# Matmuls on different parts of TensorE's array issued as neighbours in the mixers of a hybrid layer

## Chip, cores and metric

One core of one Trainium2 chip runs the whole layer in one launch. The metric is device time in microseconds (us), the median of the runs; smaller is better.

## What is computed

One layer over 512 latent tokens and 256 context tokens of 1024 channels, batch 1, in float32: a modulated RMSNorm, one input projection of width 4480, two groups of mixers, an output projection with a gated residual, a second norm, a router over 64 experts with 8 per token, a shared expert, and a final norm. The mixers are what matters here:

```python
# RWKV-7, 8 heads of 64, both directions, per token:
sa = einsum('bhvk,bhk->bhv', s, a_t)
s = s * w_t + sa[..., None] * b_t + v_t[..., None] * k_t      # state 64 x 64 per head
y = einsum('bhvk,bhk->bhv', s, r_t)
# HGRN2, 8 heads of 64, both directions, in chunks of 32 tokens:
scores = where(causal, einsum('ik,jk->ij', q * exp(cum - ref), k * exp(ref - cum)), 0)
o = scores @ v + (q * exp(cum)) @ s_prev
# modulation of both norms and of the residual gates:
mod = silu(c) @ w_mod + b_mod                                  # 1024 x 6144
```

## The kernel before

Two heads of 64 channels make a pair of 128 partitions, and there are four pairs for each kind of mixer. RWKV-7 runs in chunks of 64 tokens: 12 chunks, of which the first 4 are context and the other 8 latent, in both directions at once.

The mixers are written as Python generators, the streams. P is the projection, S the scores of RWKV-7, I the inverses of its triangular systems, A, B and C the scans over the chunks (A takes pairs 0 and 2, B pair 1, C pair 3), H and K HGRN2 (pairs 0, 1 and pairs 2, 3), M the rest of the modulation rows, U the output projection. Each stream runs from one `yield` to the next as a step, and all streams take turns. A table, PLAN, holds for each stream priorities along its steps and the number of its steps; the framework orders the instructions of each engine by these priorities and their dependences. An engine then executes its instructions in that fixed order. A wait in TensorE's queue thus holds up whatever stands behind it, of every stream.

The places that the change touches:

- `rw_scores` (stream S, matmul on line 687). For every two chunks and each head h, a matmul pair with 64 rows (the head's partitions) and 128 columns goes to one PSUM bank; DVE masks it on line 689 into the tile SC. The two heads are two steps, and they use banks 4 and 5 in turns. There are 4 pairs x 2 directions x 6 double chunks = 48 rounds of two heads.
- `rw_chain` (A, B, C). A chunk's step has four groups: the right-hand side (line 888, 64 x 64 of the array, and line 891, 128 x 64), the solve (line 902, 64 x 64), the state (line 910), and for latent chunks the output (line 926, 128 x 128, and line 928, 128 x 64). Lines 888 and 891 run over d 0 entirely and then over d 1; line 902 likewise; lines 926 and 928 alternate.
- `hgrn_pair` (H, K). For each direction, for g in (0, 2) and each head, two groups of 128 tokens make three kinds of score matmuls in one PSUM bank: lines 1115 and 1116 use 64 rows x 128 columns, line 1118 64 x 64. DVE (line 1122) and ACT (lines 1127 and 1129) bring them to SBUF. There are 4 pairs x 2 directions x 2 values of g = 16 rounds of two heads.
- `s_mod` (M). 32 loads of 512 KB of w_mod, each 256 rows x 512 columns. Each gives two matmuls with 32 array columns (line 1203) that fill one strip of 32 partitions; the four strips of a row block follow each other over four loads.

A float32 matmul shows as two records in the trace. After the mixers come norm, router and the experts, which the change does not touch.

Of the kernel before, what the change touches and what calls it, by code (L numbers as in the profile page):

```python
# [11 lines left out]
I32 = mybir.dt.int32  # L12
# [11 lines left out]
NWL, NWR = 4, 1               # buffers for the weights of experts  # L24
LAG = 2                      # loads in flight
ONPE = range(12, 44, 2)      # blocks whose rows TensorE picks, from rows on chip; the others' come by DMA
HB = 4                       # block from which on these rows are loaded
NP = 4                       # experts whose weights come before the routing is known: they rank last
# experts by size: NONE have a block of 128 slots each, NMIX 96 slots of a block, NTWO are two to a block, and the
# smallest NMIX have the other 32 slots of the former  # L30
NONE, NMIX = 18, 10
NTWO = 64 - NP - NONE - 2 * NMIX
# pairs in the output projection, in the order in which they are ready
OUT = [[('rw', 0), ('hg', 0)], [('rw', 1), ('rw', 2)], [('hg', 1), ('hg', 2)], [('hg', 3), ('rw', 3)]]
# priorities of the streams along their steps, and the number of steps; smaller ones go first
PLAN = {'W': (5, 195, 454, 106), 'P': (76, 299, 531, 185), 'E': (31, 271, 489, 172), 'O': (31, 126, 188, 169),
# [10 lines left out]
def hybrid_layer(ctx, tc, x, c, xctx, c_ctx, w_mod, b_mod, norm1_g, norm2_g, w_in, rw_conv, rw_w0, rw_w2,  # L47
# [29 lines left out]
    # ---------------------------------------------------------------- constants  # L77
# [24 lines left out]
    # masks of the chunk scores, rows (B s | K s) for d 0 and (K s | B s) for d 1, columns (A t | R t)  # L102
# [11 lines left out]
    # scan resets  # L114
# [6 lines left out]
    # masks of the 32-token blocks of HGRN2, for two heads  # L121
# [15 lines left out]
    hTh = hp.tile([128, 8, NT], FR)             # hT = hTh + hTl, each exact in float32r  # L137
# [14 lines left out]
    # conditioning vectors, then per-channel vectors, rows of 128 turned into columns  # L152
# [13 lines left out]
    lo = const.tile([128, 2, 8], F32)          # lb, 1 - lb  # L166
# [9 lines left out]
    def vectors():  # L176
# [34 lines left out]
    # adaLN: silu of the conditioning vectors as a stationary operand  # L211
# [55 lines left out]
    def banks(names):  # L267
        """PSUM in turns"""
        names = list(names)

        def get(name):
# [1630 lines left out]
```

## Time and profile before

| | |
|---|---|
| median of 3 runs | 1969.67 us (1947.13 to 1979.79) |
| span of the profiled execution | 1964.3 us |
| TensorE (PE) busy | 1777.6 us, 90% |
| DVE, ACT, POOL busy | 753.9, 618.5, 395.2 us |
| mean granted TensorE clock | 0.904 |

The profile is one execution. A row of the timeline gives the start in us, the time from the start to the last end in us, engine, line, operation, operands, shape and count; the next row's start tells when the engine came to other work. "64*128 64x128" means that 64 rows and 128 columns of the array are used and that 128 columns stream through.

### The profile page before, as it was taken

The numbers are of one execution on the slowest core, as the hardware profiler recorded it, in microseconds if no ns is written. First come the engines' busy times: TensorE is split into PE (matmuls) and PEld (weight loads), VectorE is DVE, ScalarE is ACT, GpSimd is POOL, SyncE is SP. The second block draws the span as 40 slices with busy tenths as digits, with TensorE's granted clock in tenths as the row PEclk, the third lists the DMA queues.
The fourth block names the chain that finished last, engine by engine and source line by source line (L and its number), as shares of the span: only waits on it lengthen the run. The fifth ranks groups of instructions, "written<-read, shape, count | busy, mean of one in ns | idle before, by whom it ended". The sixth has DMA issues, their size and how long they took to land. (4 is left out here: it accounts for less than half of the span.)

```text
span 1964.3 us, 25497 instructions
## 1 busy us (share of the span) xinstructions
PE 1777.6 (90%) x9675; PEld 1004.8 (51%) x9675; DVE 753.9 (38%) x1722; ACT 618.5 (31%) x1286; POOL 395.2 (20%) x372
## 2 busy tenths in 40 slices
PE   5998989999699999898999889988899999799983
PEld 2766676675577775564455443333344443433431
DVE  4566685847563344433446332111121121111113
ACT  5463535345143353421323232111121221111121
POOL 2233223313221242231230012100111110101111
PEclk9977988998579977687999989999899999899987
DMA  7313555554565354533437877995967999758975
GB/s 257 94 50 108 148 137 147 174 137 134 129 210 144 114 185 139 169 128 124 141 124 281 296 259 245 333 348 204 318 204 249 311 324 335 247 187 296 350 238 161
DMA packets 200252, 401.65 MB, mean 204 GB/s; under 512 B 41804, under 2 KB 132009, under 8 KB 175168
## 3 DMA queue, kind: packets, MB, share of 16 engines
q1 hardware_dynamic: 188768, 360.05, 53.0%
q0 software_dynamic: 11360, 39.96, 9.1%
q8 instruction: 77, 1.26, 0.3%
q14 instruction: 47, 0.39, 0.1%
HBM read 323.66 MB, written 73.15 MB: 202 GB/s over the span
## 5 line engine op out<-in xcount | busy, mean ns | idle before, releaser
L1467 PE MATMUL p_gu<-wgu,xT 128*64 128x512 f32 (+3 forms) x1104 | 424.1, 605 | 0.4 <-ACT xT L1458 0.4
L1467 PEld LDWEIGHTS p_gu<-wgu,xT 128*64 128x64 f32 (+3 forms) x1104 | 129.1, 155 | 254.0 <-issue 240.2
L1485 PE MATMUL p_y<-wd,at 128*64 128x512 f32 (+3 forms) x584 | 240.8, 636 | 4.4 <-ACT at L1480 3.0
L369 PE MATMUL p_proj<-hTh,w_hi 128*128 128x512 f32 (+1 forms) x456 | 181.5, 398 | 6.0 <-ACT w_hi L296 3.1
L370 PE MATMUL p_proj<-hTh,w_lo 128*128 128x512 f32 (+1 forms) x456 | 176.3, 388 | 3.8 <-DVE w_lo L298 3.8
L371 PE MATMUL p_proj<-hTl,w_hi 128*128 128x512 f32 (+1 forms) x456 | 177.3, 390 | 2.3 <-POOL hTl L351 1.7
L1687 POOL DMA_INDIRECT acc<-rows,li x46 | 74.3, 1616 | 463.6 <-DVE rows L1686 443.4
L1634 DVE SCALAR_TENSOR_TENSOR li<-lv,bpr 128x2 int32<-128x2 f32 x46 | 10.1, 219 | 401.1 <-DMA acc<-rows,li 287.9
L1485 PEld LDWEIGHTS p_y<-wd,at 128*64 128x64 f32 (+3 forms) x584 | 71.2, 162 | 141.8 <-issue 124.0
L1472 ACT ACTIVATE sl<-p_gu 128x256 f32<-128x256 f32 x50 | 19.2, 384 | 384.9 <-PE p_gu L1467 383.4
L1458 ACT ACTIVATE xT<-p_xg,sh2c,s2c 128x128 f32<-128x128 f32 x240 | 90.1, 461 | 110.0 <-PE p_xg L1746 109.7
L1686 DVE SCALAR_TENSOR_TENSOR rows<-p_y,lv,g2r 128x512 f32<-128x512 f32 x92 | 68.2, 746 | 147.3 <-PE p_y L1485 147.1
L369 PEld LDWEIGHTS p_proj<-hTh,w_hi 128*128 128x128 f32 x456 | 94.7, 208 | 28.4 <-issue 6.1
L371 PEld LDWEIGHTS p_proj<-hTl,w_hi 128*128 128x128 f32 x456 | 94.4, 207 | 21.7 <-issue 5.6
L370 PEld LDWEIGHTS p_proj<-hTh,w_lo 128*128 128x128 f32 x456 | 94.6, 208 | 19.6 <-issue 4.6
L1740 POOL DMA_INDIRECT xg<-h,li x30 | 31.4, 1047 | 346.6 <-issue 158.1
L1735 PE MATMUL p_xs<-sel,h2p 128*128 128x128 bf16 x1536 | 92.9, 219 | 0.0
L1735 PEld LDWEIGHTS <-h2p 128*128 128x128 bf16 x1536 | 87.4, 98 | 9.5 <-issue 9.2
L687 PE MATMUL p_sc<-AR,BK 64*128 64x128 f32 (+1 forms) x384 | 64.9, 341 | 20.0 <-DVE SC L689 9.1
L1458 ACT ACTIVATE xT<-p_xs,sh2c,s2c 128x128 f32<-128x128 f32 x128 | 48.2, 458 | 105.5 <-PE p_xs L1735 105.5
L1474 DVE TENSOR_TENSOR av<-sl,p_gu 128x256 f32<-128x256 f32 x50 | 30.1, 602 | 115.8 <-ACT sl L1472 115.8
L687 PEld LDWEIGHTS p_sc<-AR,BK 64*128 64x128 f32 x384 | 50.5, 228 | 41.3 <-issue 12.8
(520 smaller groups left out, 2716.8 us busy)
## 6 DMA issues: line engine op xcount, KB each, us to landing
wgu<-in_exp_w_gate_dram SPq DMA_DIRECT2D x64, 1024.0 KB, 6.7
wgu<-in_exp_w_up_dram SPq DMA_DIRECT2D x64, 1024.0 KB, 8.4
wd<-in_exp_w_down_dram SPq DMA_DIRECT2D x64, 1024.0 KB, 6.3
w_raw<-in_w_in_dram SPq DMA_DIRECT2D x35, 512.0 KB, 4.1
wm<-in_w_mod_dram SPq DMA_DIRECT2D x32, 512.0 KB, 3.8
pkt<-pk SPq DMA_DIRECT2D x24, 576.0 KB, 4.7
wm<-in_w_mod_dram SPq DMA_DIRECT2D x8, 1024.0 KB, 8.3
pk<-SC SPq DMA_DIRECT2D x32, 256.0 KB, 3.5
```

The source lines that it names most:

```text
L369: pe.matmul(o[k], wh[:, kt, :], hTh[:, kt, s], start=(kt == 0), stop=False)
L370: pe.matmul(o[k], wl[:, kt, :], hTh[:, kt, s], start=False, stop=False)
L371: pe.matmul(o[k], wh[:, kt, :], hTl[:, kt, s], start=False, stop=(kt == 7))
L687: pe.matmul(p3[:, i], bk[r, n + i, :], ar[r, n + i, 0:w], start=True, stop=True)
L1458: act.activation(dst[:, kt, :], v, AF.Identity, scale=s2c[:, kt:kt + 1], bias=sh2c[:, kt:kt + 1])
L1467: pe.matmul(pg[r], lhs(kt), w[0][:, :, kt * 256:kt * 256 + 256], start=(kt == 0), stop=(kt == 7))
L1474: dve.tensor_tensor(av.rearrange("s t p -> s p t"), sl.rearrange("s (p t) -> s p t", t=2), pg[:, 256:512].rearrange("s (p t) -> s p t", t= ...
L1485: pe.matmul(py[n][r], at[:, t * 128 + r.start:t * 128 + r.stop], w[1][:, t * 1024 + n * 512:t * 1024 + n * 512 + 512], start=(t == 0), sto ...
L1686: dve.scalar_tensor_tensor(yo[:, cs_], py[n], g, g2r[:, cs_], op0=OP.mult, op1=OP.mult)
L1687: pool.indirect_dma_start(out=ACC if two else ACC[0:NACC], in_=yo, in_offset=None, compute_op=OP.add, out_offset=bass.IndirectOffsetOnAxis ...
L1735: pe.matmul(pt[:, q * 128:q * 128 + 128], h2p[:, i, t, kt * 128:kt * 128 + 128], sel[:, t], start=(i == 0 and t == 0), stop=(i == 2 and t ...
L1740: pool.indirect_dma_start(out=xg.bitcast(F32), out_offset=None, in_=H2_d, in_offset=bass.IndirectOffsetOnAxis(ap=tok, axis=0))
```

## The change

In `rw_scores` both heads are issued in one step, alternating between the upper and the lower half of the array's rows, and then both are masked; both banks are taken in one step. In `rw_chain` the loops over head and direction are swapped on lines 888 and 902, so that neighbours use different halves; the matmuls with all 128 rows follow together. In `hgrn_pair` both heads are issued in one step, alternating by head, those of 64 x 64 last; then both are copied. In `s_mod` a load covers 512 rows x 256 columns, and each load feeds all four strips, with 256 columns streamed instead of 512, so that there are 8 records to a load instead of 4. The step counts in PLAN follow (S 345 to 249, H and K 153 to 129).

```diff
-        'S': (136, 309, 469, 345),
+        'S': (136, 309, 469, 249),     (H and K: 153 to 129)
 rw_scores:
-            for h in range(2):
-                r = slice(64 * h, 64 * h + 64)
-                p3 = pss("p_sc")[:, 0:2 * w].rearrange("p (i t) -> p i t", i=2)
-                for i in range(2):
+            p3s = [pss("p_sc")[:, 0:2 * w].rearrange("p (i t) -> p i t", i=2) for _ in range(2)]
+            for i in range(2):
+                for h, p3 in enumerate(p3s):
+                    r = slice(64 * h, 64 * h + 64)
                     pe.matmul(p3[:, i], bk[r, n + i, :], ar[r, n + i, 0:w], start=True, stop=True)
-                yield
+            yield
+            for h, p3 in enumerate(p3s):
                 dve.tensor_tensor(st[:, :, 0:na, h], ...)
-                yield
+            yield
 rw_chain:
-            for d in range(2):
-                for h in range(2):
+            for h in range(2):
+                for d in range(2):
                     pe.matmul(pR[r, o:o + 64], SC[rv, d, 0, h, :], W[rv, d, o:o + 64], ...)
-                if n:
-                    pe.matmul(pR[r, 0:128], AR[d][:, 0:64], S[:, d, :], start=False, stop=True)
+            if n:
+                for d in range(2):
+                    pe.matmul(pR[64 * d:64 * d + 64, 0:128], AR[d][:, 0:64], S[:, d, :], start=False, stop=True)
...
-            for d in range(2):
-                for h in range(2):
+            for h in range(2):
+                for d in range(2):
                     pe.matmul(pU[r, h * 64:h * 64 + 64], TT[r, h, :], Rs[r, h * 64:h * 64 + 64], ...)
...
                 for d in range(2):
-                    pe.matmul(pY[:, o:o + 64], S[:, d, :], AR[d][:, 64:128], start=True, stop=False)
+                    pe.matmul(pY[:, d * 64:d * 64 + 64], S[:, d, :], AR[d][:, 64:128], start=(d == 0), stop=False)
+                for d in range(2):
                     for h in range(2):
                         pe.matmul(pY[64 * h:64 * h + 64, ...], W[:, d, ...], SC[:, d, 1, h, :], ...)
 hgrn_pair:
             for g in (0, 2):
-                for h in range(2):
-                    pa = psg("p_ls")
-                    for i in range(2):
-                        pe.matmul(p0[:, i], ...)
-                        pe.matmul(p1[:, i], ...)
-                        pe.matmul(p2[kr_, i], ...)
-                    yield
-                    dve.copy_predicated(Pv, hgm[d], p0)
-                    yield
+                pas = [psg("p_ls") for _ in range(2)]
+                for i in range(2):
+                    for r, p0 in zip(hr_, p0s):
+                        pe.matmul(p0[:, i], ...)
+                    for r, p1 in zip(hr_, p1s):
+                        pe.matmul(p1[:, i], ...)
+                for i in range(2):
+                    for r, p2 in zip(hr_, p2s):
+                        pe.matmul(p2[kr_, i], ...)
+                yield
+                for h in range(2):
+                    dve.copy_predicated(Pg[:, g:g + 2, h, :], hgm[d], p0s[h])
+                yield
...
 s_mod:
-                m, g = 4 + i // 4, i % 4
-                wm = mo.tile([128, 2, 512], F32, name="wm2", bufs=3)
+                m, n, h = 4 + i // 4, i // 2 % 2, i % 2
+                wm = mo.tile([128, 4, 256], F32, name="wm2", bufs=3)
...
-                for kt in range(2):
-                    pe.matmul(pm[32 * g:32 * g + 32, :], sil[:, 2 * g + kt, :], wms[i][:, kt, :], ...)
+                for g in range(4):
+                    pe.matmul(pm[32 * g:32 * g + 32, n * 256:n * 256 + 256], sil[:, 4 * h + g, :], wms[i][:, g, :], ...)
```

## Rows read from the trace of the kernel before

**Rows 1.** The page: the span, and the granted TensorE clock in 40 slices.
```profile
span 1964.3 us, 25497 instructions
...
PEclk9977988998579977687999989999899999899987
```

**Rows 2.** Busy times by stretch: window, us, PE, PEld, DVE, ACT, POOL, clock, DMA, GB/s.
```profile
130.00:320.00 190.00, 172.45 (x949) 129.42 (x949) 124.43 (x201) 82.27 (x121) 51.76 (x34) 0.84 0.43 120
320.00:600.00 280.00, 252.32 (x1766) 188.57 (x1764) 180.99 (x394) 108.84 (x190) 82.60 (x71) 0.85 0.55 157
600.00:800.00 200.00, 196.80 (x1416) 139.76 (x1416) 78.89 (x183) 82.61 (x189) 49.11 (x80) 0.87 0.47 152
800.00:1000.00 200.00, 184.61 (x928) 104.55 (x929) 75.91 (x164) 61.67 (x138) 55.70 (x59) 0.83 0.39 131
```

**Rows 3.** Groups of PE by form: busy us, mean ns, idle before and what ended it.
```profile
L687 PE MATMUL p_sc<-AR,BK 64*128 64x128 f32 x256 | 41.6, 334 | 8.1 <-DVE SC L689 8.1
L687 PE MATMUL p_sc<-AR,BK 64*128 64x64 f32 x128 | 24.5, 353 | 11.9 <-POOL BK L637 4.3 <-DVE BK L638 3.5 <-ACT cv_b L447 3.1
L1203 PE MATMUL p_mod<-wm,sil 128*32 128x512 f32 x128 | 50.8, 789 | 2.6 <-DMA wm<-in_w_mod_dram 1.7 <-ACT mrow L1215 0.7 <-DVE y_rw L962 0.2
```

**Rows 4.** Timeline of PE: scores of one head alone, and of two heads together.
```profile
476.48 0.66 PE L687 MATMUL p_sc<-AR,BK 64*128 64x64 f32 x4
477.06 0.50 PE L370 MATMUL p_proj<-hTh,w_lo 128*128 128x512 f32 x1
...
404.11 0.72 PE L687 MATMUL p_sc<-AR,BK 64*128 64x128 f32 x8
404.76 0.50 PE L369 MATMUL p_proj<-hTh,w_hi 128*128 128x512 f32 x1
```

**Rows 5.** Timeline of PE: a right-hand side of the scan, then HGRN2's scores.
```profile
811.76 0.47 PE L888 MATMUL p_chain<-WvR,pktS 64*64 64x64 f32 x4
...
812.52 0.44 PE L888 MATMUL p_chain<-WvR,pktS 64*64 64x64 f32 x4
...
813.25 0.48 PE L1115 MATMUL p_ls<-e,k 64*128 64x128 f32 x2
...
814.10 0.48 PE L1115 MATMUL p_ls<-e,k 64*128 64x128 f32 x2
```

**Rows 6.** Timeline of PE: modulation rows of three loads, then a scan's output.
```profile
972.56 1.93 PE L1203 MATMUL p_mod<-wm,sil 128*32 128x512 f32 x12
974.54 0.43 PE L926 MATMUL p_chain<-pktS 128*128 128x64 f32 x2
974.91 0.34 PE L928 MATMUL p_chain<-pktS,WvR 128*64 128x64 f32 x4
975.17 0.43 PE L926 MATMUL p_chain<-pktS 128*128 128x64 f32 x2
...
975.80 1.12 PE L1269 MATMUL p_out<-wo,y_rw 128*128 128x512 f32 x2
```

**Rows 7.** Timeline of PE: four records of line 888 at the lower clock.
```profile
741.01 0.69 PE L888 MATMUL p_chain<-Wv,pkt 64*64 64x64 f32 x4
```

**Rows 8.** Timeline of PE: the first modulation rows, whose order alternates strips.
```profile
36.09 1.94 PE L332 MATMUL p_mod<-wm,sil 128*32 128x512 f32 x16
```

**Rows 9.** What empties the score banks: engine, count, ns min/median/max, first and last.
```profile
L689 DVE TENSOR_TENSOR SC<-p_sc,mks x96: 271/412/426, 128.1 to 525.4; 128x256 f32<-128x256 f32 x64, 128x128 f32<-128x128 f32 x32
...
L1122 DVE COPY_PREDICATED Pg<-hgm,p_ls x32: 440/444/448, 604.7 to 991.4; 128x256 f32<-128x256 uint8 x32
...
L1127 ACT ACTIVATE Pg<-p_ls x64: 197/215/218, 605.2 to 992.1; 32x64 f32<-32x64 f32 x64
...
L1129 ACT ACTIVATE Pg<-p_ls x32: 258/272/273, 605.6 to 992.3; 64x128 f32<-64x128 f32 x32
```

**Rows 10.** DMA issues: count, KB each, median us from issue to landing.
```profile
w_raw<-in_w_in_dram SPq DMA_DIRECT2D x35, 512.0 KB, 4.1
wm<-in_w_mod_dram SPq DMA_DIRECT2D x32, 512.0 KB, 3.8
```

More of the change, by code (lines that the diff above doesn't have):

```diff
@@ L882, in rw_chain @@
             W = loaded['W', n // 2][:, n % 2]
-            for d in range(2):
-                r = slice(64 * d, 64 * d + 64)
-                rv = slice(64 - 64 * d, 128 - 64 * d)
-                for h in range(2):
+            for h in range(2):
+                for d in range(2):
+                    r = slice(64 * d, 64 * d + 64)
+                    rv = slice(64 - 64 * d, 128 - 64 * d)
                     o = h * 64
@@ L898, in rw_chain @@
             yield
-            for d in range(2):
-                r = slice(64 * d, 64 * d + 64)
-                for h in range(2):
+            for h in range(2):
+                for d in range(2):
+                    r = slice(64 * d, 64 * d + 64)
                     pe.matmul(pU[r, h * 64:h * 64 + 64], TT[r, h, :], Rs[r, h * 64:h * 64 + 64],
@@ L924, in rw_chain @@
                 for d in range(2):
-                    o = d * 64
-                    pe.matmul(pY[:, o:o + 64], S[:, d, :], AR[d][:, 64:128], start=True, stop=False)
+                    pe.matmul(pY[:, d * 64:d * 64 + 64], S[:, d, :], AR[d][:, 64:128], start=(d == 0), stop=False)
+                for d in range(2):
                     for h in range(2):
-                        pe.matmul(pY[64 * h:64 * h + 64, o:o + 64], W[:, d, h * 64:h * 64 + 64],
-                                  SC[:, d, 1, h, :], start=False, stop=True)
+                        pe.matmul(pY[64 * h:64 * h + 64, d * 64:d * 64 + 64], W[:, d, h * 64:h * 64 + 64],
+                                  SC[:, d, 1, h, :], start=False, stop=(d == 1))
                 yield
@@ L1106, in hgrn_pair @@
             for g in (0, 2):
-                for h in range(2):
-                    r = slice(64 * h, 64 * h + 64)
-                    pa = psg("p_ls")
-                    p0 = pa[:, 0:256].rearrange("p (g i) -> p g i", g=2)
-                    p1 = pa[:, 256:384].rearrange("p (g n b) -> p g n b", g=2, n=2)
-                    p2 = pa[:, 384:512].rearrange("p (g i) -> p g i", g=2)
-                    for i in range(2):
-                        gs_ = slice((g + i) * 128, (g + i) * 128 + 128)
+                pas = [psg("p_ls") for _ in range(2)]
+                p0s = [pa[:, 0:256].rearrange("p (g i) -> p g i", g=2) for pa in pas]
+                p1s = [pa[:, 256:384].rearrange("p (g n b) -> p g n b", g=2, n=2) for pa in pas]
+                p2s = [pa[:, 384:512].rearrange("p (g i) -> p g i", g=2) for pa in pas]
+                hr_ = [slice(64 * h, 64 * h + 64) for h in range(2)]
+                for i in range(2):
+                    gs_ = slice((g + i) * 128, (g + i) * 128 + 128)
+                    for r, p0 in zip(hr_, p0s):
                         pe.matmul(p0[:, i], k0_[r, gs_], e1_[r, gs_], start=True, stop=True)
+                    for r, p1 in zip(hr_, p1s):
                         pe.matmul(p1[:, i], ke_[r, CTX + gs_.start:CTX + gs_.stop], qe4[r, g + i, odd::2, :],
                                   start=True, stop=True)
+                for i in range(2):
+                    for r, p2 in zip(hr_, p2s):
                         pe.matmul(p2[kr_, i], k2[r, g + i].rearrange("p n b -> p (n b)"),
                                   q2[r, g + i].rearrange("p n b -> p (n b)"), start=True, stop=True)
-                    yield
+                yield
+                for h in range(2):
+                    dve.copy_predicated(Pg[:, g:g + 2, h, :], hgm[d], p0s[h])
+                yield
+                for h in range(2):
                     Pv = Pg[:, g:g + 2, h, :]
-                    dve.copy_predicated(Pv, hgm[d], p0)
-                    yield
                     for n in range(2):
@@ L1126, in hgrn_pair @@
                         c0 = 64 * n + 32 * odd
-                        act.activation(Pv[r0:r0 + 32, :, c0:c0 + 32], p1[r0:r0 + 32, :, n, :], AF.Copy)
+                        act.activation(Pv[r0:r0 + 32, :, c0:c0 + 32], p1s[h][r0:r0 + 32, :, n, :], AF.Copy)
                     c0 = 32 * qsec
-                    act.activation(Pv[kr_, :, c0:c0 + 64], p2[kr_], AF.Copy)
-                    yield
+                    act.activation(Pv[kr_, :, c0:c0 + 64], p2s[h][kr_], AF.Copy)
+                yield
             for i0, i1 in ((0, 3), (3, 5)):
@@ L1197, in s_mod @@
             pm = psm("p_mod2")
-            for g in range(4):
-                i = 4 * (m - 4) + g
+            for q in range(4):
+                i, n, h = 4 * (m - 4) + q, q // 2, q % 2
                 loads(i + 2)
                 yield
-                for kt in range(2):
-                    pe.matmul(pm[32 * g:32 * g + 32, :], sil[:, 2 * g + kt, :], wms[i][:, kt, :], start=(kt == 0),
-                              stop=(kt == 1))
-                if g == 1:
+                for g in range(4):
+                    pe.matmul(pm[32 * g:32 * g + 32, n * 256:n * 256 + 256], sil[:, 4 * h + g, :], wms[i][:, g, :],
+                              start=(h == 0), stop=(h == 1))
+                if q == 1:
                     store()
```

3 lines of the change are left out of this document (2 added, 1 removed), and 4 rows, old and new, of the table PLAN.

## Prediction

> **What bounds the kernel now.** I read the page first, then the busy times by stretch, the groups of PE by form, and the timeline of PE where the touched lines run. The span is 1964.3 us [rows 1]. The touched matmuls lie between 130 and 1000 us, and there PE is the busiest engine in every stretch: 172.5 of 190, 252.3 of 280, 196.8 of 200 and 184.6 of 200 us, 806.2 of 870 [rows 2]. DVE comes next with 124.4 and 181.0 us up to 600 us (65%) and 39% after; ACT stays at 41% or less before 600 us and 36% after [rows 2]. So PE idles 64 us in all, and the reader should see that work taken from PE's queue has few other owners of the time. Two things are not in the busy share. Ends of matmuls are modelled, so a lone block is "busy" while its results drain. And the granted clock is 0.84, 0.85, 0.87 and 0.83 there: with only the levels 1.2 and 2.4 GHz, (1 - clock) x 2 of each stretch is at the lower one, 61 + 84 + 52 + 68 = 265 us of 870 [rows 2]. Four records of line 888 take 0.69 us at the lower level against 0.44 at the higher [rows 5, 7], 1.6 times as long. With 30% of the time at the lower level, a price taken at the full clock counts 1 / (0.7 + 0.3 / 1.6) = 1.13 times on average.
>
> **The change part by part.** PE's arithmetic stays; what changes is what runs side by side.
>
> *Scores of RWKV-7.* One head's four records keep PE 0.58 us until other work starts; eight records, two heads on the two row halves, keep it 0.65 us [rows 4]. Two heads thus cost what one costs. The 384 records hold PE 41.6 + 24.5 = 66.1 us [rows 3]. Afterwards, 48 rounds x 0.72 us (the eight's own time) x 1.13 = 39. Gain 27 us; some heads already run side by side, as the row with eight records shows, which is why it isn't half.
>
> *Right-hand side of the scan.* A chunk takes 813.25 - 811.76 = 1.49 us, one direction after the other; the second direction alone takes 813.25 - 812.52 = 0.73 [rows 5]. The two directions use different rows and columns on line 888 and different columns on line 891, so I let both run in 0.74. That is 0.75 x 44 chunks with a state x 1.13 = 37 us. From below it is nothing, if the two do not run together.
>
> *Solve.* Line 902 has the same small tiles, only reordered. I cost it at nothing, and the other two groups of a step cover any shift.
>
> *Output of the scan.* 975.80 - 974.54 = 1.26 us now, with four changes of shape [rows 6]: 0.37 for a record pair of line 926, 0.26 for four of line 928. Two changes fall away. Between 0 and 0.5 us I take 0.25: x 32 x 1.13 = 9 us.
>
> *HGRN2's scores.* One group of one head takes 814.10 - 813.25 = 0.85 us [rows 5], so a round of two heads and two groups takes 3.4. With the heads side by side, as the RWKV-7 scores of the same shape run now [rows 4], it is 1.7; the 64 x 64 ones go last, which saves a change of shape, so 1.5. That is 1.9 x 16 x 1.13 = 34 us. From below it is nothing.
>
> *Modulation.* 128 records hold PE 50.8 us [rows 3]. Sixteen records of 512 columns on alternating strips take 1.94 us [rows 8], 0.12 each, entry included; half the columns should take 0.06, so eight records take 0.49. From above stand the 0.72 us of eight records of line 687 [rows 4], as eight short records carry more of the entry each. I take 0.69, near that end. 32 x 0.69 x 1.13 = 25 us, a gain of 26. The gain is less where loads already joined, twelve records in 1.98 us [rows 6]; that is in the 50.8. Pieces of 1 KB instead of 2 KB change the loads little: those of w_raw, of the same 512 KB in pieces of 512 bytes, land in 4.1 us against 3.8 [rows 10]. DMA is at 0.39 to 0.47 there [rows 2], and the number of buffers, the 32 loads in SP's queue and the place of the stores among them stay.
>
> Sum: 27 + 37 + 9 + 34 + 26 = 133 us of PE's queue. How much of it reaches the end? At most all: PE waits only 64 of 870 us. At least nothing, if the scans' and HGRN2's dependences fill the room. Up to 600 us DVE would rise from 65% to about 72% (305 of 470 - 45 us), and it works in chains behind PE, so half should pass there; after 600 us nobody but PE is above 40%, and two thirds should pass. A good third of the sum lies in the first part (the scores and the first chunks of the scans), so I take 0.6 of the whole: 80 us. From the profiled 1964.3 that leaves 1884; the median of the runs is 5.4 above the profiled span, so 1890. The experts after the mixers keep their time and start earlier.
>
> **Rivals.**
>
> *Both banks at once (little change).* Until now one head's bank is emptied while the other is filled. Now a round takes both, and the next round waits for both: two masks of 0.41 us [rows 9], 48 x 0.82 = 39 us, and for HGRN2 two copies of 0.44, four of 0.215 and two of 0.272 us, 2.3 x 16 = 37 us. Everything behind the waiting matmul in PE's queue, of every stream, waits too. For it: the two masked tiles are the same two banks, and PE already waits 8.1 us for SC [rows 3]. Against it: other streams' matmuls stand between two rounds. If it holds in full, (133 - 76) x 0.6 = 34 us remain: 1935. The Trainium skill, "TensorEngine Tiling (Array Packing)", section Performance Considerations (PSUM Bottleneck), says that tiling speeds up TensorE but not the emptying of PSUM, and that the copy may become the limit. By that rule, this is the case to expect; the emptying engines at 65% and 41% do not show it yet.
>
> *The neighbours don't meet (little change).* The order comes from priorities, and other streams' matmuls may still be put between those of one step. With half of the gain gone, 133 / 2 x 0.6 = 40 us: 1930. For it: the lone head in [rows 4] shows how a block is set between others; against it, that one was a step of its own.
>
> *The clock (slower).* Falls to the lower level come in stretches of small matmuls, such as that of [rows 7], where PE changes among scan and scores without a wait. Shorter bursts with the same waits between them could leave PE less active and lengthen the 265 us. Each us more at the lower level loses 1 - 1 / 1.6 = 0.375 us. The gain of 80 is used up at 213 us more; slower by 2% (39 us) needs 317 us more, 582 of the 870, and gives 2009. Against it: the same columns in less time are more activity, not less, and the stretch with four strips at once [rows 8] lies in a slice with 0.9 of the clock [rows 1]. The Trainium skill, "TensorE: Matmul & The Clock Gate", the section on the oscillation in real kernels, tells of gaps that bring the lower clock again and again; the trace agrees that the clock falls often in the mixers, clock 0.83 to 0.87, and doesn't show which way this change moves it.
>
> **How the numbers follow.** Forecast, 1890: 0.66. Both banks, 1935: 0.14. Neighbours that don't meet, 1930: 0.09. Clock, 2009 at its deciding point: 0.11. A measurement of this kernel tells about 2% (39 us) from no change. Faster by more: the 0.66 and 0.02 of the banks' case in part. Slower by more: 0.09 of the clock's. Within: the rest, 0.23. The range begins where all of the sum arrives, 1970 - 133 = 1837, and reaches over the two middle cases to 1960, where a tenth of the sum arrives and which leaves out little but the clock's case. The likeliest case alone has 1837 to 1925.
>
> **What would show it.** Line 687 should stand in the timeline as x8 nearly everywhere, and hold about 39 us; lines 1115 to 1118 as one run of 24 in about 1.5 us; line 888 as one run of 8 in the time that 4 take now; line 1203 as runs of 8 in 0.7 us. PE's busy time between 130 us and the end of the mixers should fall by over 100 us, and the first router matmul should come 60 to 100 us earlier. I am wrong if PE's busy time falls and its waits for SC, Pg and W rise by the same amount (banks), if the runs stay x4 (neighbours), if the clock of the mixers falls below 0.75 (clock), or if the part after the mixers changes its length.

## The result and the profile after

The changed kernel takes 1907.61 us (median of 4 runs, 1900.4 to 1915.17) against 1964.77 before: a ratio of 0.973 [0.9667, 0.9792]. By the ratio that is 53 us less, and the time is inside the predicted range. The forecast was 1890. Ratios here and below are taken from runs in the chip's faster state alone (for joined_mixed these are two of its four runs, and its profile is of one of the others). From the page of the changed kernel's profiled execution, the span and the granted clock in 40 slices (answers [rows 1]):

```profile
span 1913.4 us, 25717 instructions
...
PEclk9977789798685899778999999989899999999987
```

Busy times by stretch: window, us, PE, PEld, DVE, ACT, POOL, clock, DMA, GB/s (answers [rows 2]; the mixers now end at 977 us):

```profile
130.00:320.00 190.00, 173.35 (x934) 128.12 (x933) 124.41 (x199) 79.11 (x117) 52.61 (x35) 0.78 0.44 121
320.00:600.00 280.00, 239.16 (x1768) 178.06 (x1768) 183.78 (x400) 115.00 (x198) 81.43 (x71) 0.80 0.56 158
600.00:800.00 200.00, 186.13 (x1647) 142.96 (x1645) 91.29 (x211) 102.21 (x223) 60.57 (x95) 0.83 0.55 176
800.00:954.00 154.00, 137.69 (x860) 78.31 (x861) 66.65 (x144) 42.40 (x106) 41.15 (x43) 0.84 0.47 161
```

The clock is lower in three of the four stretches than in [rows 2]: 0.78, 0.80, 0.83 and 0.84 against 0.84, 0.85, 0.87 and 0.83. The transposes ahead of the router are the first work behind the mixers. First the row of before, then the one of after (start of the first and the last after the durations):

```profile
L1505 PE MATMUL p_h<-ident,h x32: 272/273/278, 1033.0 to 1048.1; 128*128 128x128 f32 x32
```
```profile
L1517 PE MATMUL p_h<-ident,h x32: 272/273/421, 976.7 to 997.2; 128*128 128x128 f32 x32
```

They start 56.3 us earlier. The span is 50.9 us shorter, so the rest of the kernel takes 5.4 us more, and the gain arises ahead of the router.

Groups of PE by form (busy us, mean ns, idle before and what ended it; answers [rows 3]). Lines 688, 1121 to 1127 and 1215 stand for 687, 1115 to 1118 and 1203 of before:

```profile
L688 PE MATMUL p_sc<-AR,BK 64*128 64x128 f32 x256 | 48.8, 383 | 10.4 <-DVE SC L691 10.4
L688 PE MATMUL p_sc<-AR,BK 64*128 64x64 f32 x128 | 18.9, 338 | 12.9 <-POOL BK L637 6.7 <-DVE BK L638 4.4 <-DVE SC L691 1.8
L1121 PE MATMUL p_ls<-e,k 64*128 64x128 f32 x128 | 24.1, 355 | 1.4 <-ACT Pg L1140 1.1
L1215 PE MATMUL p_mod<-wm,sil 128*32 128x256 f32 x256 | 23.6, 440 | 1.8 <-DMA wm<-in_w_mod_dram 1.8
```

The modulation fell from 50.8 to 23.6 us, as costed. The scores went from 66.1 to 67.7: they did not fall.

**Where PE's queue went.** For the following table I took the starts of all PE instructions from 100 us to the router and gave each stretch from one start to the next, less the idle time, to the line that started it. So it is worked out from the trace, at both clock levels together. "Right-hand side" is lines 888 and 891 of before with their counterparts, "lower" the time at the lower clock level, (1 - clock) x 2.

| us | before | after | change |
|---|---|---|---|
| scores | 59.5 | 61.2 | +1.7 |
| right-hand side | 75.3 | 45.6 | -29.7 |
| solve | 21.8 | 21.7 | 0 |
| output of the scan | 42.7 | 34.2 | -8.5 |
| HGRN2's scores | 65.0 | 33.3 | -31.7 |
| modulation | 49.4 | 22.3 | -27.1 |
| PE idle | 69.7 | 93.6 | +23.9 |
| lower | 271.5 | 314.6 | +43.1 |

The touched lines free 97 us, 95 net of the scores' rise; idle time takes 24 back, and the untouched lines run some 15 us longer, about what 43 us more at the lower level cost at the prediction's 0.375 us each (16 us). 95 - 24 - 15 = 56.

What the side-by-side issue looks like where it works: timeline of PE in after, a right-hand side of both directions, one round of HGRN2's scores, and one load of the modulation, all at the higher level (start, duration, count):

```profile
710.37 0.45 PE L891 MATMUL p_chain<-WvR,pktS 64*64 64x64 f32 x8
710.75 0.44 PE L895 MATMUL p_chain<-pktS 128*64 128x128 f32 x4
...
833.09 0.64 PE L1215 MATMUL p_mod<-wm,sil 128*32 128x256 f32 x8
833.66 0.66 PE L930 MATMUL p_chain<-pktS 128*128 128x64 f32 x4
...
870.07 0.49 PE L1121 MATMUL p_ls<-e,k 64*128 64x128 f32 x4
870.39 0.34 PE L1123 MATMUL p_ls<-qe,ke 64*128 64x64 f32 x4
870.56 0.44 PE L1121 MATMUL p_ls<-e,k 64*128 64x128 f32 x4
870.84 0.34 PE L1123 MATMUL p_ls<-qe,ke 64*128 64x64 f32 x4
871.25 0.45 PE L1127 MATMUL p_ls<-q,k 64*64 64x64 f32 x8
871.63 0.71 PE L914 MATMUL p_chain<-WvR,pktS 128*128 128x128 f32 x4
```

Eight records of the right-hand side last 0.45 us, where four lasted 0.44 or 0.47 [rows 5]. Counted over the trace, 42 of the 48 right-hand sides stand as such a run of eight, and a whole right-hand side of a chunk with a state takes 0.75 us at the higher level instead of 1.47 (medians). Twenty-four records of HGRN2 take 871.63 - 870.07 = 1.56 us; 7 of the 16 rounds stand unbroken, 4 of them in five stretches of one shape as here. A load of the modulation takes 0.57. And where it doesn't work, the scores in after:

```profile
389.74 0.66 PE L688 MATMUL p_sc<-AR,BK 64*128 64x64 f32 x4
390.32 0.50 PE L369 MATMUL p_proj<-hTh,w_hi 128*128 128x512 f32 x1
...
401.90 0.71 PE L688 MATMUL p_sc<-AR,BK 64*128 64x128 f32 x8
402.54 0.39 PE L369 MATMUL p_proj<-hTh,w_hi 128*128 128x256 f32 x1
...
404.68 0.71 PE L688 MATMUL p_sc<-AR,BK 64*128 64x128 f32 x4
405.32 0.43 PE L930 MATMUL p_chain<-pkt,S 128*128 128x64 f32 x2
```

Eight records hold PE 0.64 us, and four still come alone, for 0.58 and 0.64. The price of four records or eight is the same, as [rows 4] had it; but many rounds are still split.

### The profile page after: what moved, and what is told of

Read it like the earlier page. It is cut to its first block, busy times and chain, and to the rows that moved or that the text cites. A ratio compares the mean times of both kernels' runs of the same rounds, so it can differ in the third digit from the quotient of the medians.

```text
span 1913.4 us, 25717 instructions
## 1 busy us (share of the span) xinstructions
PE 1701.0 (89%) x9803; PEld 968.1 (51%) x9803; DVE 756.5 (40%) x1722; ACT 620.3 (32%) x1289; POOL 391.9 (20%) x372
## 5 line engine op out<-in xcount | busy, mean ns | idle before, releaser
L688 PE MATMUL p_sc<-AR,BK 64*128 64x128 f32 (+1 forms) x384 | 65.8, 368 | 23.4 <-DVE SC L691 12.2
```

The lines of the kernel that those rows point to most:

```text
L688: pe.matmul(p3[:, i], bk[r, n + i, :], ar[r, n + i, 0:w], start=True, stop=True)
```

## Experiments: which part pays

The forecast's theory is that each part frees queue time and 0.6 of it arrives. The rivals are that the parts don't meet, that banks hold them up, and that the clock takes the gain back. Each part of the change was first put into the kernel before alone.

**only_chain**: the loops of the scan alone.

```diff
-            for d in range(2):
-                for h in range(2):
+            for h in range(2):
+                for d in range(2):
                     pe.matmul(pR[r, o:o + 64], ...)
-                if n:
-                    pe.matmul(pR[r, 0:128], ...)
+            if n:
+                for d in range(2):
+                    pe.matmul(pR[64 * d:64 * d + 64, 0:128], ...)
...
```

> The kernel before with the change to the scans alone. Theory 'each part pays by itself, 0.58 of what it frees': 38 us of the queue freed (right-hand sides 75 to 46, outputs 43 to 34 us), 22 us of the run, ratio 0.989. Rival 'given back': the queue time falls as much, the run by under 5 us.

Measured: 1920.28, ratio 0.9832 [0.9754, 0.991], 33 us. The right-hand side holds the queue 42.2 us instead of 75.3, the output 32.9 instead of 42.7: 43 us freed, 0.77 of them arrive (the interval of the ratio is 18 to 48 us).

**only_hgrn**: HGRN2's scores alone, both heads in one step, alternating.

```diff
-                for h in range(2):
...
-                    for i in range(2):
-                        pe.matmul(p0[:, i], ...)
-                        pe.matmul(p1[:, i], ...)
-                        pe.matmul(p2[kr_, i], ...)
...
+                for i in range(2):
+                    for r, p0 in zip(hr_, p0s):
+                        pe.matmul(p0[:, i], ...)
+                    for r, p1 in zip(hr_, p1s):
+                        pe.matmul(p1[:, i], ...)
+                for i in range(2):
+                    for r, p2 in zip(hr_, p2s):
+                        pe.matmul(p2[kr_, i], ...)
...
```

> The kernel before with the change to HGRN2's scores alone (and the step counts of its streams). Theory 'each part pays by itself, 0.58 of what it frees' (56 of 97 us in the changed kernel): the scores of HGRN2 go from 65 to about 33 us of TensorE's queue, the run is 18 us shorter, ratio 0.99. Rival 'what is freed is given back to the clock and to waits unless the neighbours' parts fall too': the queue time falls as much, the run by under 5 us, and the time at the lower clock rises from 272 us.

Measured: 1933.13, 0.9864 [0.9826, 0.9902], 27 us. Queue time 65.0 to 31.0: 34 freed, 0.79 arrive (the interval is 19 to 34 us).

**chain_hgrn**: these two edits together.

```diff
+ the edit of only_chain
+ the edit of only_hgrn
```

> The change to the scans and to HGRN2's scores alone; the scores of RWKV-7 and the modulation rows as before. Measured so far: HGRN2 alone 1933 us, the scans alone 1920, the modulation alone 1968, all three 1886, before 1960. Theory 'the modulation's part gives back through the clock': leaving it out costs nothing, 1880 to 1892 us, ratio 0.96 to 0.966, and the time at the lower clock up to the router falls from the 275 us of all three. Rival 'it pays once the queue is short': its 27 us come back at 0.58, 1902 us, ratio 0.971.

Measured: 1904.71, 0.9695 [0.9652, 0.9738], 60 us, the sum of 33 and 27. These two parts alone are as fast as the whole change. The queue time freed is 79 us, so 0.76 of it arrives, and the interval (51 to 68 us) leaves out the forecast's 0.6 unless a part of the gain is the clock's (below). The time is that of the rival, by which the modulation's part pays something once the queue is short, not that of the theory.

**only_mod**: the loads and the order of the modulation alone.

```diff
-                wm = mo.tile([128, 2, 512], F32, name="wm2", bufs=3)
+                wm = mo.tile([128, 4, 256], F32, name="wm2", bufs=3)
...
-                for kt in range(2):
-                    pe.matmul(pm[32 * g:32 * g + 32, :], ...)
+                for g in range(4):
+                    pe.matmul(pm[32 * g:32 * g + 32, n * 256:n * 256 + 256], ...)
```

> The kernel before with the change to the modulation rows alone (four strips to a load, 256 columns, pieces of 1 KB). Theory 'each part pays by itself': 27 us of the queue freed (49 to 22 us), 16 us of the run, ratio 0.992. Rival 'given back': the run by under 5 us. Waits of TensorE for these loads stay under 4 us by both.

Measured: 1967.99, 1.0063 [1.002, 1.0106]: slower. The queue time fell from 49.4 to 26.7 us all the same, and the run is 12 us longer.

**only_scores**: the scores alone.

```diff
-            for h in range(2):
-                p3 = pss("p_sc")...
-                for i in range(2):
+            p3s = [pss("p_sc")... for _ in range(2)]
+            for i in range(2):
+                for h, p3 in enumerate(p3s):
                     pe.matmul(p3[:, i], ...)
```

> The kernel before with the change to RWKV-7's scores alone. Leaving it out of the changed kernel gave 1886 instead of 1908 us. Theory 'both banks at once delay this stream wherever it stands': 1975 to 1985 us, ratio 1.008 to 1.013, the last score later than 517 us, where the kernels with the old scores have it at 511 to 529. Rival 'it only hurts beside the other parts': 1955 to 1965, ratio 1.0.

Measured: 1994.94, 1.0144 [1.009, 1.0197]: 28 us slower. The scores hold the queue 61.3 us (59.5 before), and 389 us lie at the lower level up to the router (272 before). That is more than either side of the expectation, and two us of queue don't explain it; the clock does, as the section on the modulation shows over all runs.

**no_scores**: the whole change without that of the scores.

```diff
-            p3s = [pss("p_sc")... for _ in range(2)]
-            for i in range(2):
-                for h, p3 in enumerate(p3s):
+            for h in range(2):
+                p3 = pss("p_sc")...
+                for i in range(2):
                     pe.matmul(p3[:, i], ...)
```

> The changed kernel with the scores of RWKV-7 as before: one head a step, banks in turns, and the old step count of that stream; all else as changed. In the changed kernel the scores hold TensorE 61.2 us against 59.5 before. Theory 'the scores part is idle' (the heads still don't meet): 1908 us, ratio to before 0.97, within 10 us of the changed kernel. Rival 'the scores part pays': their gain, put at 27 us of the queue, is lost, of which 0.6 reaches the end: 1924 us, ratio 0.98. Second rival 'both banks cost': faster than the changed kernel by 10 us or more, below 1898, with fewer and shorter waits of the scores for the masks than 12.2 us.

Measured: 1885.85, 0.9655 [0.9599, 0.9711]. The interval overlaps that of the whole change (0.9667 to 0.9792), but with only_scores beside it the sign is plain: this part costs time. In medians it costs 22 us here, by the ratios 0.0075, or 15 us. The signs of the second rival came: 1886 us, and waits for the masks of 9.2 us in 5 against 12.2 in 10. But 3 us of waits are not 15 to 22, and scores_joined below waits longer and is faster.

## Experiments: why the scores' edit didn't pair, and what pairing is worth

I counted in the traces how PE's score records stand. Unbroken runs of exactly eight (a whole round of two heads) were 14 before and are 21 after; runs of exactly four (half a round) were 48 and are 30. Longer runs hold several rounds (one of 48 records before, three with 60 in all after). So one step issues both heads, yet what lands in the queue is often half a round. Each head needs its own bank, which the mask of the round before frees; the masks come one after the other, so the heads become ready at different times, and the planner, the framework's ordering by priorities and dependences, fills the gap with other streams. The round still needs both before its masks. If that is so, a dependence that holds the first head back until the second bank is free should make the pairs meet.

**scores_joined**: after, and the first score matmul of a round waits for the second mask of the round before (but for the first round of each pair and direction).

```diff
-                    pe.matmul(p3[:, i], bk[r, n + i, :], ar[r, n + i, 0:w], start=True, stop=True)
+                    mm = pe.matmul(p3[:, i], bk[r, n + i, :], ar[r, n + i, 0:w], start=True, stop=True)
+                    if i == h == 0 and n:
+                        tc.add_manual_dep(mm.ins, masked.ins.name, ..., reason="both banks")
...
-                dve.tensor_tensor(st[:, :, 0:na, h], ...)
+                masked = dve.tensor_tensor(st[:, :, 0:na, h], ...)
```

> The changed kernel with one dependence more: the first score matmul of a round waits for both masks of the round before, so that both heads become ready together and stand side by side in TensorE's order. Theory 'the cost is that the two heads don't meet': the scores hold the queue under 50 us instead of 61, the run is under 1900 us. Rival 'the cost is the wait for both banks': the queue time falls likewise, but waits of the scores for the masks rise over 12 us and the run is 1908 us or more.

Measured: 1873.58 (1857.17 to 1880.62, 5 runs), 0.9557 [0.9506, 0.9607], 34 us under the change as it was. Groups of PE by form, scores_joined:

```profile
L688 PE MATMUL p_sc<-AR,BK 64*128 64x128 f32 x256 | 29.6, 335 | 15.7 <-DVE SC L694 15.6
L688 PE MATMUL p_sc<-AR,BK 64*128 64x64 f32 x128 | 16.3, 328 | 9.6 <-DVE BK L638 4.1 <-POOL BK L637 3.4 <-ACT KBs L718 1.2
```

The scores are busy 45.9 us instead of 67.7, and from start to start 42.0 instead of 61.2. Runs of exactly eight went from 21 to 33, runs of four from 30 to 13. PE's waits for the masks, first of before, then of after, then of scores_joined (total us, times, longest):

```profile
PE p_sc L687 <- DVE SC L689: 9.1, 5, 4.0
```
```profile
PE p_sc L688 <- DVE SC L691: 12.2, 10, 5.2
```
```profile
PE p_sc L688 <- DVE SC L694: 15.6, 8, 7.4
```

The explicit wait for both banks costs 3.4 us more waiting than the change had, and returns 19 us of queue. So waiting for both banks is cheap, and not waiting for both was the fault. The 34 us are not all queue time, though: most of them are the clock's (below).

**joined_no_mod**: scores_joined with the modulation of before.

```diff
-                for g in range(4):
-                    pe.matmul(pm[32 * g:32 * g + 32, n * 256:n * 256 + 256], ...)
+                for kt in range(2):
+                    pe.matmul(pm[32 * g:32 * g + 32, :], ...)
```

> The kernel of 1874 us (all of the change and the dependence) with the modulation rows as before. Theory 'the modulation's part gives back to the clock': 1866 to 1880 us, ratio 0.952 to 0.96, time at the lower clock up to the router at 219 us or less. Rival 'with the queue shorter it pays': 0.58 x 27 = 16 us longer, 1890 us, ratio 0.964.

Measured: 1884.19, 0.9583 [0.9541, 0.9625]. Against chain_hgrn (0.9695 [0.9652, 0.9738]), which differs by the scores alone, it is 0.0112 or 22 us better, with the intervals apart: that is what paired scores are worth here. Against scores_joined (0.9557) the modulation's edit is not told from nothing. In time the run lies between the theory and its rival, and its 253 us at the lower level up to the router speak against the theory, which had 219 at most.

**joined_alone**: the kernel before with the scores' edit and the dependence, and nothing else.

```diff
+ the edit of only_scores
+ the dependence of scores_joined
```

> The kernel before with RWKV-7's scores in rounds of two heads and the one dependence that makes both heads ready together; nothing else of the change. Without the dependence the same part alone gave 1995 us, ratio 1.014. Theory 'the rounds pay only when the heads meet': the scores hold the queue 40 to 45 us instead of 61, ratio 0.975 to 0.99, 1915 to 1945 us. Rival 'the dependence helps only beside the other parts': ratio 1.0 or more.

Measured: 1960.03 (10 runs), 0.9988 [0.9951, 1.0026]. It takes away the loss of only_scores (1.0144), but gains nothing, though its scores hold the queue 42.0 us too. The expected 1 to 2.5% was wrong: 18 us of PE's queue free nothing alone, and are worth 22 us when the scans and HGRN2 are paired. The clock accounts for most of that: over all runs joined_alone has 38 us more at the lower level than before, 14 us of time, while the two kernels whose difference is 22 us have the same (table below). What lowers it here is open.

**joined_by_head**: scores_joined, with HGRN2's heads one behind the other. Both are still issued in one step, neighbours in the queue, with both banks taken at once.

```diff
-                for i in range(2):
-                    for r, p0 in zip(hr_, p0s):
-                        pe.matmul(p0[:, i], ...)
-                    for r, p1 in zip(hr_, p1s):
-                        pe.matmul(p1[:, i], ...)
-                for i in range(2):
-                    for r, p2 in zip(hr_, p2s):
-                        pe.matmul(p2[kr_, i], ...)
+                for r, p0, p1, p2 in zip(hr_, p0s, p1s, p2s):
+                    for i in range(2):
+                        pe.matmul(p0[:, i], ...)
+                        pe.matmul(p1[:, i], ...)
+                    for i in range(2):
+                        pe.matmul(p2[kr_, i], ...)
```

> The kernel of 1874 us with HGRN2's scores of both heads still in one step, but one head after the other in TensorE's order, each head's 64 x 64 ones last. Theory 'what counts is that they stand close, not that they alternate': side by side all the same, as line 902 and the scores of before run; the queue time of HGRN2's scores stays under 38 us (33 now), the run within 8 us of 1874. Rival 'alternating is what makes them run together': 55 us or more of the queue, 13 us longer, 1887 us, ratio 0.963.

Measured: 1916.79 (1907.84 to 1932.34), 0.9747 [0.9678, 0.9816], 43 us over scores_joined. Timeline of PE, joined_by_head, a round at the lower level with its second head's twelve records in full, and then after, both heads' twenty-four at the same level:

```profile
565.39 0.79 PE L1124 MATMUL p_ls<-e,k 64*128 64x128 f32 x2
...
567.90 0.79 PE L1124 MATMUL p_ls<-e,k 64*128 64x128 f32 x2
568.49 0.52 PE L1125 MATMUL p_ls<-qe,ke 64*128 64x64 f32 x2
568.81 0.74 PE L1124 MATMUL p_ls<-e,k 64*128 64x128 f32 x2
569.34 0.52 PE L1125 MATMUL p_ls<-qe,ke 64*128 64x64 f32 x2
569.80 0.68 PE L1128 MATMUL p_ls<-q,k 64*64 64x64 f32 x4
570.41 0.58 PE L917 MATMUL p_chain<-Wv,pkt 128*128 128x128 f32 x1
```
```profile
595.83 0.80 PE L1121 MATMUL p_ls<-e,k 64*128 64x128 f32 x4
596.42 0.53 PE L1123 MATMUL p_ls<-qe,ke 64*128 64x64 f32 x4
596.74 0.74 PE L1121 MATMUL p_ls<-e,k 64*128 64x128 f32 x4
597.27 0.53 PE L1123 MATMUL p_ls<-qe,ke 64*128 64x64 f32 x4
597.73 0.69 PE L1127 MATMUL p_ls<-q,k 64*64 64x64 f32 x8
598.35 0.58 PE L914 MATMUL p_chain<-Wv,pkt 128*128 128x128 f32 x1
```

One head takes 570.41 - 567.90 = 2.51 us, two take 598.35 - 595.83 = 2.52: the second head is free if its records stand beside those of the same shape. Over all rounds the queue time is 62.7 us by head against 32.8 in scores_joined, and 65.0 before the change. These sums mix the clock levels. Unbroken rounds of 24 records at the higher level, first of before, then of joined_by_head (first row and the row behind the round):

```profile
983.53 0.49 PE L1115 MATMUL p_ls<-e,k 64*128 64x128 f32 x2
...
986.89 1.13 PE L1269 MATMUL p_out<-wo,y_rw 128*128 128x512 f32 x2
```
```profile
667.47 0.48 PE L1124 MATMUL p_ls<-e,k 64*128 64x128 f32 x2
...
670.28 0.50 PE L369 MATMUL p_proj<-hTh,w_hi 128*128 128x512 f32 x1
```

A round takes 3.36 us in before, 2.81 by head and 1.42 to 1.56 in after. So putting each head's 64 x 64 records last saves 0.55 us, and letting the heads share each stretch of one shape saves the rest. The run changes two things at once: the heads no longer alternate, and a round has ten stretches of one shape (the same part of the array, the same columns streamed) instead of five. Rows of other lines point to the second, as within a stretch the order of the halves makes no difference: eight score records hold PE 0.65 us in before, where one head's step follows the other's, and 0.65 in after and in scores_joined, where the heads alternate (medians at the higher level); the solve, which the change only reordered, holds the queue 21.8 and 21.7 us. The 43 us also hold a share of the clock: over all runs joined_by_head has 72 us more at the lower level than scores_joined, 27 us of time.

**joined_mixed**: scores_joined, with the 64 x 64 matmuls behind each group of 128 tokens instead of last.

```diff
                     for r, p1 in zip(hr_, p1s):
                         pe.matmul(p1[:, i], ...)
-                for i in range(2):
                     for r, p2 in zip(hr_, p2s):
                         pe.matmul(p2[kr_, i], ...)
```

> The kernel of 1874 us with HGRN2's scores alternating by head, but the 64 x 64 ones behind each group of 128 tokens as before instead of all last: three changes of shape within a round instead of one. Theory 'a change of shape costs about 0.2 us': 16 x 2 x 0.2 x 1.13 = 7 us more of the queue, 40 us instead of 33, run within 8 us of 1874. Rival 'one shape together is the main part': 50 us or more of the queue, 1884 us or more.

Measured: 1874.02 (1851.05 to 1886.59), 0.9457 [0.9383, 0.953]. The median is that of scores_joined and the intervals overlap: putting those of one shape last makes no difference in time that can be told. Its queue time for HGRN2's scores is 38.4 us against 32.8, and an unbroken round at the higher level takes 1.71 us against 1.42 with two more changes between 64*128 and 64*64 of the array, 0.15 us each.

## Experiment: why the modulation's gain didn't arrive

**mod_twice**: only_mod, with the first half of each sum computed three times, twice for nothing, so that twice the columns go through the array in the same places.

```diff
+                for g in [g for _ in range(2 - 2 * h) for g in range(4)]:
+                    pe.matmul(pm[32 * g:32 * g + 32, n * 256:n * 256 + 256], ..., start=True, stop=True)
                 for g in range(4):
                     pe.matmul(pm[32 * g:32 * g + 32, n * 256:n * 256 + 256], ..., start=(h == 0), stop=(h == 1))
```

> The kernel with the modulation's change alone (1968 us), in which every first half of a modulation row's sum is computed three times, twice of them for nothing into the place that the third overwrites: twice the columns of this part, about 23 us more of TensorE's queue. Theory 'what this part frees is given back to the clock, so work put back costs nothing': within 8 us of 1968, the time at the lower clock up to the router falls below 295 us from 307. Rival 'TensorE's queue': 0.58 x 23 = 13 us longer or more, 1981 us, ratio 1.013.

Measured: 1955.17, 0.9959 [0.9922, 0.9996]. More work, 40.8 us of queue instead of 26.7, and it is faster than only_mod (1.0063 [1.002, 1.0106]), with the intervals apart. The expectation had it within 8 us of 1968; its 256 us at the lower level up to the router are below the 295 that the theory named. The stretches in which most of the modulation runs, in before, only_mod and mod_twice (the clock is the third number from the end):

```profile
700.00:800.00 100.00, 97.63 (x616) 62.08 (x613) 47.61 (x119) 46.92 (x99) 33.43 (x54) 0.80 0.50 168
800.00:900.00 100.00, 91.42 (x457) 56.35 (x456) 35.31 (x74) 33.61 (x73) 30.98 (x36) 0.72 0.37 123
```
```profile
700.00:800.00 100.00, 97.44 (x598) 66.63 (x599) 45.10 (x108) 43.02 (x92) 28.92 (x51) 0.65 0.50 160
800.00:900.00 100.00, 91.13 (x491) 59.43 (x491) 35.52 (x78) 33.72 (x73) 31.57 (x37) 0.69 0.38 124
```
```profile
700.00:800.00 100.00, 98.62 (x736) 68.38 (x736) 48.34 (x114) 47.69 (x104) 31.85 (x53) 0.76 0.51 167
800.00:900.00 100.00, 88.77 (x595) 55.14 (x595) 35.46 (x86) 31.13 (x71) 30.09 (x36) 0.84 0.49 163
```

At the lower level lie (0.20 + 0.28) x 200 = 96 us of before, 132 of only_mod and 80 of mod_twice. PE is about as busy in all three. 36 us more at 0.375 us each are 14 of the 23 us that only_mod frees. That added work shortens the time is shown by the medians.

That it does so through the clock would rest on one profile of each, but the record has more: for every run it lists the span and the mean granted clock, and (1 - clock) x 2 x span is the run's time at the lower level, here over the whole kernel. Means over the runs behind the ratios; the runs of one kernel scatter by 11 to 29 us around them (standard deviation):

| kernel | runs | us at the lower level | more than before, x 0.375 | time against before, by ratio |
|---|---|---|---|---|
| before | 49 | 370 | | |
| only_mod | 9 | 429 | +22 | +12 |
| mod_twice | 9 | 368 | -1 | -8 |
| only_scores | 4 | 470 | +38 | +28 |
| joined_alone | 10 | 408 | +14 | -2 |
| chain_hgrn | 6 | 341 | -11 | -60 |
| no_scores | 4 | 354 | -6 | -68 |
| after | 4 | 416 | +17 | -53 |
| joined_no_mod | 6 | 343 | -10 | -82 |
| scores_joined | 5 | 338 | -12 | -87 |
| joined_by_head | 4 | 410 | +15 | -50 |

Among the 49 runs of before, each us more at the lower level goes with 0.43 us more of span, close to the forecast's 0.375. So the clock accounts for the 12 us that only_mod loses and covers the 20 us between it and mod_twice (23 us of clock; of the 14 us of queue put back little shows). It accounts for the loss of only_scores, and for 29 of the 34 us between after and scores_joined. The queue and the clock are two effects of the same edits, and only the first was in the forecast's sum. Less the clock's part, 0.61 to 0.79 of the queue time that the touched lines free arrives in the last six kernels of the table; in chain_hgrn it is (60 - 11) / 79 = 0.62. In only_chain and only_hgrn, both with 343 us at the lower level, it is 0.5. What in these edits lowers the clock is not shown.

## Why the prediction was right, and where not

The total came within 18 us of the forecast, partly by luck: errors of both signs met. The forecast's shares (0.6 of each term) beside what the runs give, by ratios x 1964.8 us (the three steps go from before over chain_hgrn and no_scores to after, so they add up):

| part | queue, predicted | queue, measured | time, predicted | time, measured |
|---|---|---|---|---|
| scans and HGRN2 | 80 | 70 (79 in chain_hgrn) | 48 | 60 |
| modulation | 26 | 27 | 16 | 8 (no_scores against chain_hgrn), not told from 0; -12 alone |
| scores | 27 | -2 | 16 | -15 (after against no_scores); -28 alone |
| sum | 133 | 95 | 80 | 53 |

*Scans and HGRN2: right.* The right-hand side was put at 37 and measured 30, the output 9 and 8.5, HGRN2 34 and 32. The directions do run together, as the step said: 0.45 us for eight records of line 888's kind, 0.44 for four of line 891's. The share of 0.6 looks too small beside the 0.76 that arrive of chain_hgrn's 79 us (0.65 to 0.87). But 11 of its 60 us are the clock's, with 29 us less at the lower level, and the queue's own share is 0.62. The factor 1.6 for the lower level fits the small runs of line 888; an unbroken round of HGRN2 takes 1.8 times as long (1.42 and 2.52 us), which would raise the prices by 2%.

*The scores: wrong.* The step that failed is "afterwards, 48 rounds x 0.72 us": the price of eight records held (0.64 in after), but not that every round would be eight. The rival "the neighbours don't meet" was right on this part, and its objection, that the lone head of [rows 4] "was a step of its own", was the mistake: in one step the matmuls are still separate to the planner, and each is placed when its own bank is free. The rival "both banks at once" had the right tile and the wrong sign. Its price, 39 us of waiting, did not appear (12.2 us of waits for SC after, 9.1 before), and making the wait explicit gained 34 us. The two us of queue that the part costs are not its 15 us of time; over all runs after has 62 us more at the lower level than no_scores, and that is 23 us. The Trainium skill ("TensorEngine Tiling (Array Packing)", Performance Considerations) says that the copy may become the limit after a fourfold speed-up of TensorE; with two halves at once it is not the limit here, as even scores_joined waits only 15.6 us for the masks in 130 to 930 us.

*The modulation: the queue right, the arrival wrong.* 27 us left the queue, and no pair of kernels shows a gain from it that can be told: +12 us alone, -8 beside scans and HGRN2, -5 beside paired scores. Alone, the clock takes more than the queue gives (22 us); beside the other parts the time at the lower level is the same with and without it to within 13 us, and why no more of the 27 us arrives there is open.

*The clock: a rival that came in part.* The time at the lower level rose by 43 us in the profile and by 46 us over all runs, where slower by 2% would have needed 317. The scores' edit alone (1.0144) and the modulation's alone (1.0063) raised it by 100 and 59 us. The objection "the same columns in less time are more activity" fell with only_mod. The scans' and HGRN2's edits went the other way: 343, 343 and 341 us in only_chain, only_hgrn and chain_hgrn against 370, over all runs. So it isn't shorter bursts as such that lower the clock, and which ones do is open.

*What would show it.* Held: line 888 as runs of eight in the time of four, and modulation in 0.57. Held in part: HGRN2's 24 in 1.42 to 1.56 us at the higher level, where they stand as five unbroken stretches (4 of 16 rounds). Not held: scores as eight nearly everywhere, and 39 us. PE's busy time up to the router fell by 80 us instead of over 100 (100 us to the router less idle: 863 to 783). The router comes 56 us earlier, just under the 60 to 100.

The best version measured is scores_joined, 1873.58 us, 34 us under the change as it was; joined_mixed is as fast.

## What to carry to other kernels

To run two small matmuls side by side it isn't enough to issue them in one step: check in the trace that they stand next to each other, within one stretch of the same shape, and where a planner places them, give both the same moment of readiness (one dependence on the later bank). Price each part of such a change in the kernel alone and with the others, as parts that free the queue can give it back through the clock: work out the time at the lower level for every run, not for the one in the profile. The share of freed queue time that arrived here was 0 for one part alone and 0.76 for two others, and the clock is a good part of that difference.

## What the runs showed of the hardware

- In these rows what stands on the other half of the array is free, and what stands on the same half is not. Runs of 2, 4 and 8 score records in before hold PE 0.42, 0.64 and 0.65 us (64x128, medians at the higher level; the first two are one head, the third is two). In HGRN2 one head's 12 records and both heads' 24 take 2.51 and 2.52 us at the lower level, if both heads share their five stretches of one shape; with ten stretches, one head behind the other, the 24 take 570.41 - 565.39 = 5.02. The Trainium skill ("TensorEngine Tiling (Array Packing)", Tiling Modes, Key Properties) says that a change of the mode drains TensorE, while different tiles run in parallel; the trace agrees on both, with 2.51 against 2.52 us for the tiles and 0.15 us for a change between 64*128 and 64*64 in joined_mixed at the higher level.
- Taking time from PE's queue can cost as much as it saves: 23 us less queue at the same number of matmul columns gave 1.0063, and adding useless columns gave 0.9959, with 429 and 368 us at the lower level over nine runs each, and 370 in before. The Trainium skill ("TensorE: Matmul & The Clock Gate", HAM oscillation) puts falls of the clock down to gaps of PE; here PE is busy 97 to 99% of 700 to 800 us by the profile in before, only_mod and mod_twice, at clocks of 0.80, 0.65 and 0.76, so gaps don't tell them apart.
- The clock of the same code differs from profile to profile: 0.84 in 130 to 320 us before, 0.89 and 0.87 in only_mod and mod_twice, which change no line that runs there. That is 61, 42 and 49 us at the lower level, so a clock difference of some 20 us in one profile proves nothing. Over the whole kernel the 49 runs of before lie between 334 and 410 us, so means over many runs decide.
